# One hybrid decoder block on one core: key halves spread by DMA, sums of h one pair per head, and an earlier emptying of the turned heads

## The chip, the cores and the metric

The program runs on one core of one Trainium2 chip. The metric is the device time of the whole program in microseconds, the median of several executions. Besides these times there is a profile of one execution, with a record of every instruction on every engine: TensorE (PE, with its weight loads shown apart as PEld), VectorE (DVE), ScalarE (ACT), GpSimd (POOL), and SyncE (SP), which issues nearly all DMAs.

## The reference, cut to what matters

The block works on 1024 positions of width 1024, all in float32. The part that the change touches is the differential attention with its four heads:

```python
h = rms_norm(x, g_mix)
proj = h @ w_in                       # q1, q2, k1, k2, va, qr, kr, vr, gr, gate_a, gate_r
s1 = einsum(q1, k1) * scale + bias    # per head, 64 wide, causal, ALiBi
s2 = einsum(q2, k2) * scale + bias
a  = (softmax(s1) - lam * softmax(s2)) @ va
a  = rms(a) * g_diff_sub * (1 - lam_init)
...
merged = sigmoid(gate_a) * (a @ w_diff_proj) + sigmoid(gate_r) * (r @ w_ret_proj)
x = x + merged @ w_out
...
x = x + (silu(zg) * zu) @ w_down      # zg, zu: causal depthwise convolution of rms_norm(x) @ w_up
```

## The kernel before

**Numbers in two halves.** A float32 operand of a matmul is kept as a rounded high half (`hi`, type fp32r) and the rest (`lo`). A product is the sum of three matmuls, hi·hi, hi·lo and lo·hi. ACT makes the high half by a copy, DVE or POOL makes the low half by a subtraction. The normalized input h lies transposed in 16 tiles `hT[0][k]`, `hT[1][k]` (high and low halves, k from 0 to 7).

**Queries and keys.** For each head h, `queries_keys(h)` runs two products over all of h, one for the queries and one for the keys, each in two halves c of 512 positions (`gemm`, PSUM tag "g" with two buffers). The product's 128 rows hold q1 and q2 of the head, or k1 and k2, 64 rows each. For the scores, the kernel stacks the two halves of the query on the 128 partitions: `qs[0]` holds q1's high half on partitions 0 to 63 and its low half on 64 to 127; `qs[1]` has q2, turned over. A score is then two matmuls, against a tile with the key's high half on both groups of 64 partitions and one with the key's low half on both. `keys` (L476 to L481) makes those tiles from PSUM: for each of k1 and k2, ACT copies the high half to the low and the top 64 partitions (L479), and DVE subtracts twice, once for each group of partitions (L481).

**Attention.** `attention(h)` runs over eight blocks of 128 queries in the order 3, 7, 6, 5, 4, 2, 1, 0. For each, PE makes scores (L502, PSUM tag "x"), DVE adds the bias and takes the minimum (L507), ACT takes the exponential (L512), DVE mixes the two softmaxes (L515 to L517), PE turns the result by transposes (L525), ACT empties it (L527), PE multiplies by the values (L530), and DVE and ACT finish (L532, L534).

**Sums of h.** `h_sums` (L571) is the preparation for a seven-product scheme that later replaces eight block products. For each of four pairs of blocks (k, k + 4) it adds high and low halves (two additions of 128x1024, L288 through `plus`), forms four differences of 128x512 (L285 through `sub`) in tiles `ta` (tag "vo", 6 buffers) and `tb` (tag "br", 9 buffers), and stores both to DRAM as `t_saved` (two DMAs, L584). `h_side` (L588) later loads the stored parts back and splits them; with p = 5 it puts them over the second half of `hT[.][k]`.

**What sets the order.** In this first part the order on each engine's queue, the SP queue of DMAs included, is worked out when the program is built, by a planner: program order gives the priority, a simulated time line says when an instruction can run, and later work fills gaps. A tile's buffer has to be free before its first writer may run. Within the shared tags the tiles of the sums stand in program order between those of the heads: an even head takes six "br" buffers (two queries, four keys), an odd head two "br" and four "c". The outer loop (L707 to L717) calls `attention(h)`, `queries_keys(h + 1)`, after head 0 also `h_sums()`, then the last head and the products for the retention's queries and keys (`retention_product`, tag "br" as well), which keep PE supplied during attention.

**Steps by hand.** From L727 on, the work of PE, DVE, ACT and POOL is ordered by hand: `issue` walks a list of steps. For each step i it issues loads for step i + 9, sums for i + 4, the high half of the weights for i + 3 (ACT), the low half for i + 2 (DVE), and then step i's `pre` list, its matmuls `mm`, and its `post` list. A step is twelve matmuls of 128x512. In the last of the steps for the gates, the attention's output is turned: `turn_a(h)` (L795) makes eight transposes into two PSUM buffers of tag "b" (there are two), and `finish_a(h)` (L799) empties them, two ACT copies for the high half (L803) and two DVE operations for the low half (L805). `n_gates` is 84: `turn_a(0..3)` stand in the `post` lists of steps 77 to 80 and `finish_a(0..3)` in those of steps 78 to 81 (L902 to L906). The products with `w_diff_proj` (`ps_pa`) begin at step 84.

Of the kernel before, what the change touches and what calls it, by code (L numbers as in the profile page):

```python
# [11 lines left out]
F32 = mybir.dt.float32  # L12
F32R = mybir.dt.float32r
AF = mybir.ActivationFunctionType
ALU = mybir.AluOpType
# [120 lines left out]
def hybrid_block(ctx: ExitStack, tc: tile.TileContext, units, xT, wall, lams, pars, consts, dist, out):  # L136
    nc = tc.nc
# [5 lines left out]
    def t4(tag, name, dt=F32, shape=(P, 1024)):  # L143
        return tp.tile(list(shape), dt, tag=tag, name=name, bufs=BUFS[tag])
# [137 lines left out]
    HK = KB // 2  # L282

    def sub(out, a, b, engine=nc.vector):
        engine.tensor_tensor(out, a, b, op=ALU.subtract)  # L285

    def plus(out, a, b, engine=nc.vector):
        engine.tensor_tensor(out, a, b, op=ALU.add)  # L288

    def copy(out, a):  # L290
        nc.scalar.activation(out, a, AF.Copy)  # L291
# [34 lines left out]
    steps, index, behind = [], {}, []  # L326
# [26 lines left out]
    with ExitStack() as first:  # L353
# [3 lines left out]
        def psum(tags, name):  # L357

            turn[0] += 1
            return pp.tile([P, 512], F32, tag=tags[turn[0] % len(tags)], name=name)  # L360
# [8 lines left out]
        for k in range(KB):  # L369
# [3 lines left out]
            for c in range(0, S, 512 if k == 0 else S):  # L373
                cs = slice(c, c + (512 if k == 0 else S))
# [8 lines left out]
            for st in range(NST):  # L383
                a = [t[:, st * P : (st + 1) * P] for t in u[k]]
                b = [t[:, k % 2 * 256 : (k % 2 + 1) * 256] for t in w]
# [16 lines left out]
        for st in range(NST):  # L402
            ps = psum("gx", f"ps_va1_{st}")[:, 0:256]
# [18 lines left out]
        for k in range(KB):  # L422
            xt = t4("s", f"xn{k}")
            nc.sync.dma_start(out=xt, in_=xT[k * P : (k + 1) * P, :])
            for c in range(2):
                cs = slice(c * 512, (c + 1) * 512)
# [23 lines left out]
        def gemm(name, tags, nm, done, engine=nc.vector):  # L450

            w = weight(name, engine=engine)
            for c in range(2):
                ps = psum(tags, f"ps{nm}_{c}")
                channel_major(ps, w, of_h, KB, c)
                done(slice(c * 512, (c + 1) * 512), ps)
# [4 lines left out]
        low, top = slice(0, HD), slice(HD, P)  # L461

        def queries_keys(h):
            sc = -(HD**-0.5) / SLOPES[h]
            qs = [t4("br", f"q{m}_{h}", F32R) for m in range(2)]
            tag = "c" if h % 2 else "br"
            ks = [[t4(tag, f"k{e}{m}_{h}", F32R) for e in range(2)] for m in range(2)]

            def queries(cs, ps):
                for q, a, b in ((qs[0], low, top), (qs[1], top, low)):  # L470
                    nc.scalar.activation(q[a, cs], ps[a], AF.Copy, scale=sc)
                    nc.vector.scalar_tensor_tensor(
                        q[b, cs], ps[a], sc, q[a, cs].bitcast(F32), op0=ALU.mult, op1=ALU.subtract
                    )

            def keys(cs, ps):  # L476
                for (kh, kl), a in zip(ks, (low, top)):
                    for b in (low, top):
                        nc.scalar.activation(kh[b, cs], ps[a], AF.Copy)  # L479
                    for b in (low, top):  # L480
                        nc.vector.tensor_tensor(kl[b, cs], ps[a], kh[a, cs].bitcast(F32), op=ALU.subtract)  # L481

            gemm(("q", h), "g", f"q{h}", queries, nc.gpsimd)
            gemm(("k", h), "g", f"k{h}", keys, nc.gpsimd)
            return qs, ks
# [58 lines left out]
        def spill(name, i, t):  # L544
            if name == "vr":
                spilled[name, i] = values[:, i, :]
            elif name in ("qr", "kr"):
                spilled[name, i] = queries_and_keys[:, i + (0 if name == "qr" else 2), :]
            else:
                spilled[name, i] = dram.tile([P, S], F32, name=f"{name}_saved{i}")  # L550
            nc.sync.dma_start(out=spilled[name, i], in_=t)
# [6 lines left out]
        def retention_product(name, p):  # L558
            t = t4("br", f"{name}{p}")
            gemm((name, p), "g", f"{name}{p}", lambda cs, ps: copy(t[:, cs], ps), nc.gpsimd)  # L560
            spill(name, p, t)
# [6 lines left out]

        t_saved = []

        def h_sums():  # L571

            for k in range(HK):
                a, b = t4("vo", f"ta{k}"), t4("br", f"tb{k}")
                for t, e in ((a, k), (b, k + HK)):
                    plus(t, hT[0][e].bitcast(F32), hT[1][e].bitcast(F32))
                b11, b12, b21, b22 = a[:, 0:512], a[:, 512:], b[:, 0:512], b[:, 512:]
                sub(b11, b12, b11)
                sub(b12, b22, b12)
                sub(b22, b22, b11)  # L580
                sub(b21, b21, b22)
                t_saved.append([dram.tile([P, S], F32, name=f"t_saved{e}_{k}") for e in range(2)])
                for t, d in zip((a, b), t_saved[k]):
                    nc.sync.dma_start(out=d, in_=t)  # L584
# [3 lines left out]
        def h_side(p, k, tag=None):  # L588

            if tag:  # L590
                t = t4(tag, f"ht{p}_{k}", F32R)
                hi, lo = t[:, 0:512], t[:, 512:]
            else:
                hi, lo = (t[k][:, second_half] for t in hT)
            e, cs = {5: (0, first_half), 7: (0, second_half), 4: (1, first_half), 6: (1, second_half)}[p]
            nc.sync.dma_start(out=lo.bitcast(F32), in_=t_saved[k][e][:, cs])
            split(lo.bitcast(F32), hi, lo)
            h_sides[p, k] = hi, lo
# [109 lines left out]
        for h in range(NH - 1):  # L708
            attention(h, *qk)
            qk = queries_keys(h + 1)  # L710
            if h == 0:
                h_sums()
        attention(3, *qk, (3, 7, 6))
        level = tc.cur_priority
        for name in ("qr", "kr"):
            for p in range(2):
                retention_product(name, p)  # L717
        for k in range(HK):
            h_side(5, k)
        for p, tag in ((6, "br"), (7, "br")):  # L720
# [20 lines left out]
        def at_step(i, *ops):  # L741
            steps[i].post.extend(ops)
# [36 lines left out]
        def scale_heads(o, r):  # L779

            nc.vector.tensor_tensor(o, o, r.rearrange("p (a b) -> p a b", b=1).broadcast_to([P, 8, DV]), op=ALU.mult)
# [113 lines left out]
        n_gates = len(steps)  # L895
# [7 lines left out]
        for h in range(NH):  # L903
            at_step(18 + h, lambda h=h: scale_heads(oa[h], rstd_a[:, h * NST : (h + 1) * NST]))
            at_step(n_gates - 7 + h, partial(turn_a, h))
            at_step(n_gates - 6 + h, partial(finish_a, h))  # L906


        MERGED = ("br",) * 5 + ("s", "s", "vo")
# [47 lines left out]
        for n in range(2 * NH):  # L957
            h, c = n // 2, n % 2
# [610 lines left out]
def build(units, arrays):  # L1569
    import concourse.bacc as bacc  # L1570

    nc = bacc.Bacc("TRN2", target_bir_lowering=False, num_devices=1)
    args = [nc.dram_tensor(f"in_{n}", a.shape, mybir.dt.from_np(a.dtype), kind="ExternalInput").ap() for n, a in arrays.items()]
    out = nc.dram_tensor("out_0", (D, S), F32, kind="ExternalOutput").ap()
    with tile.TileContext(nc, schedule_with_timeline_sim=True) as tc:
        hybrid_block(tc, units, *args, out)
    return nc
# [9 lines left out]
```

## Time and profile before

| | |
|---|---|
| Time, median of 3 executions | 1434.86 us (1434.17 to 1435.17) |
| The profiled execution's own time | 1434.84 us |
| Its span, first to last instruction | 1433.0 us |
| PE busy | 1368.6 us, 96% of the span |
| DVE busy | 1068.0 us, 75% |
| ACT busy | 703.4 us, 49% |
| DMA, mean over the span | 131 GB/s |

The profiled execution is an ordinary one: its time lies within the range of the others, and some 1.8 us of it lie outside the span. A view by windows gives, for a stretch of time, how long each engine was busy, how many instructions it ran, the clock that TensorE was granted (1.00 is full speed) and the share of the DMA engines. A PE that is busy at a clock of 0.5 does half the work. Matmuls overlap in the records, so the pace of PE is read from the distance between starts, not from the length of one.

### The profile page before, as it was taken

To read this page: it belongs to the slowest core of one execution; us is meant where nothing else is said; L and a number is where in the kernel's file an instruction comes from. 1 tells how busy PE (TensorE), PEld (TensorE's weight loads), DVE (VectorE), ACT (ScalarE), POOL (GpSimd) and SP (SyncE) were. 2 spreads that over 40 slices of the span, in tenths; PEclk is the share of its full clock that TensorE was granted. 3 is DMA by queue.
4 is the path that set the end of the run, shared out by engine and by line. 5 is a ranking of instruction groups with operands and counts; after the bars stand their busy time and mean duration, and the time that the engine had idled before them with its cause. 6 is when DMAs were issued, how large, how long until landed. Compare 5 with 4: busy or idle time off the path is not lost.

```text
span 1433.0 us, 18055 instructions
## 1 busy us (share of the span) xinstructions
PE 1368.6 (96%) x6472; PEld 1134.0 (79%) x6472; DVE 1068.0 (75%) x1699; ACT 703.4 (49%) x1318; POOL 154.3 (11%) x92
## 2 busy tenths in 40 slices
PE   7899899989999998999998989999999999999996
PEld 7887788878888886788776767888888888888885
DVE  6759765675655553467968989888988899897876
ACT  6544665564454434221445465455555556444452
POOL 6711001000000000000000012111111112200000
PEclk9999999999999999999989999999999999999997
DMA  7313101314334332635324134434433365943223
GB/s 250 125 45 121 56 16 45 137 70 143 137 125 136 108 110 81 251 138 180 153 100 148 59 113 159 133 122 136 139 126 125 125 228 195 331 165 103 94 90 118
DMA packets 81018, 187.55 MB, mean 131 GB/s; under 512 B 8320, under 2 KB 18944, under 8 KB 80928
## 3 DMA queue, kind: packets, MB, share of 16 engines
q1 hardware_dynamic: 80736, 185.74, 37.8%
q8 instruction: 51, 0.84, 0.2%
q0 software_dynamic: 192, 0.66, 0.1%
q14 instruction: 39, 0.32, 0.1%
HBM read 136.81 MB, written 49.55 MB: 130 GB/s over the span
## 4 chain that ended last, share of the span: by engine, by line
PE 42%; DVE 7%; ACT 1%; issue 1%; DVEq 0%; ACTq 0%
PE up L276 24%; PE wd L276 14%; PE wo L276 4%; DVE wf L285 1%; DVE f L285 1%; DVE x L1461 1%; DVE y L1381 1%; DVE ssum L228 1%; DVE x L1230 1%; DVE x L288 1%; DVE x L285 0%; ACT f L291 0%; DVE zg L288 0%; DVE raw_zg L285 0%; DVE wwo L285 0%
## 5 line engine op out<-in xcount | busy, mean ns | idle before, releaser
L276 PE MATMUL up<-f,wf 128*128 128x512 f32 x1848 | 424.8, 391 | 9.2 <-DVE wf L285 3.4
L276 PEld LDWEIGHTS up<-f,wf 128*128 128x128 f32 x1848 | 345.3, 188 | 88.1 <-DVE wf L285 6.4
L276 PE MATMUL wd<-awd,wwd 128*128 128x512 f32 (+1 forms) x960 | 212.2, 383 | 0.0
L276 PEld LDWEIGHTS wd<-awd,wwd 128*128 128x128 f32 x960 | 176.0, 189 | 35.4 <-issue 0.5
L285 POOL TENSOR_TENSOR t12g<-y 128x512 f32<-128x512 f32 x11 | 19.8, 1796 | 673.3 <-DVE y L1391 538.4
L276 PE MATMUL wo<-awo,wwo 128*128 128x512 f32 x336 | 83.2, 407 | 7.4 <-DVE awo L285 7.1
L276 PEld LDWEIGHTS wo<-awo,wwo 128*128 128x128 f32 x336 | 64.9, 196 | 24.8 <-DVE awo L285 10.1
L512 ACT ACTIVATE s<-s,row 128x512 f32<-128x512 f32 (+7 forms) x64 | 49.5, 773 | 26.7 <-DVE row L507 26.2
L1381 DVE SCALAR_TENSOR_TENSOR y<-zg,par,y 128x1022 f32<-128x1022 f32 (+1 forms) x44 | 58.6, 1333 | 2.9 <-ACT y L1378 2.9
L502 PE MATMUL pss<-k,q 128*128 128x512 f32 (+2 forms) x192 | 52.8, 371 | 5.6 <-DVE row L507 5.5
L288 DVE TENSOR_TENSOR zg<-zg,up 128x512 f32<-128x512 f32 x44 | 30.2, 685 | 37.0 <-PE up L276 34.6
L1381 DVE SCALAR_TENSOR_TENSOR y<-zu,par,y 128x1022 f32<-128x1022 f32 (+1 forms) x44 | 56.1, 1277 | 0.0
L291 ACT ACTIVATE zg<-up 128x512 f32<-128x512 f32 x44 | 26.1, 596 | 58.5 <-PE up L276 58.5
L285 DVE TENSOR_TENSOR awd<-act_in,awd 128x512 fp32r<-128x512 f32 x77 | 53.7, 697 | 0.0
L507 DVE CUSTOM_DVE_ANT_0 s<-pss,dist_t 128x512 f32<-128x512 f32 (+3 forms) x64 | 37.0, 587 | 21.1 <-PE pss L502 19.7
L291 ACT ACTIVATE awd<-act_in 128x512 fp32r<-128x512 f32 x77 | 47.5, 616 | 0.3 <-DVE wf L285 0.2
L276 PE MATMUL ps_pa<-a,wpa 128*128 128x512 f32 x192 | 46.0, 394 | 0.0
L206 PE MATMUL psq<-hT,hi_q 128*128 128x512 f32 x128 | 43.2, 415 | 2.5 <-ACT hi_q L163 1.7
L291 ACT ACTIVATE zu<-up 128x512 f32<-128x512 f32 x44 | 26.2, 596 | 39.2 <-PE up L276 39.1
L276 PE MATMUL ps_pr<-r,wpr 128*128 128x512 f32 x192 | 43.7, 389 | 0.0
L291 ACT ACTIVATE wwd<-wdv 128x512 fp32r<-128x512 f32 x33 | 20.9, 632 | 46.1 <-PE wd L276 37.1
L530 PEld LDWEIGHTS po<-va,at 128*128 128x128 f32 x288 | 38.1, 195 | 6.2 <-ACT at L527 4.1
(367 smaller groups left out, 2822.9 us busy)
## 6 DMA issues: line engine op xcount, KB each, us to landing
act_in<-act SPq DMA_DIRECT2D x77, 256.0 KB, 2.9
act<-y SPq DMA_DIRECT2D x55, 256.0 KB, 2.2
raw_zg<-in_wall SPq DMA_DIRECT2D x22, 512.0 KB, 3.4
raw_zu<-in_wall SPq DMA_DIRECT2D x22, 512.0 KB, 4.1
x<-in_x SPq DMA_DIRECT2D x15, 512.0 KB, 7.8
act<-t12g SPq DMA_DIRECT2D x22, 256.0 KB, 2.0
wdu<-in_wall SPq DMA_DIRECT2D x22, 256.0 KB, 4.8
wdv<-in_wall SPq DMA_DIRECT2D x22, 256.0 KB, 5.7
```

Source lines behind the costliest of these rows:

```text
L206: nc.tensor.matmul(ps, w, a, start=i == 0, stop=i == n - 1)
L228: engine.tensor_tensor(self.ssum, self.ssum, sq, op=ALU.add)
L276: nc.tensor.matmul(ps[:, cols], w[:, x * 512 + at : x * 512 + at + P], a[y][:, cols], start=start and i == 0, stop=stop and i == n - 1, sk ...
L285: engine.tensor_tensor(out, a, b, op=ALU.subtract)
L288: engine.tensor_tensor(out, a, b, op=ALU.add)
L291: nc.scalar.activation(out, a, AF.Copy)
L502: nc.tensor.matmul(ps[:, : max(n, 256)], qs[m][:, i * P : (i + 1) * P], k[:, c : c + max(n, 256)], start=e == 0, stop=e == 1,)
L507: nc.vector.tensor_tensor_reduce(s[:, c : c + n], ps[:, :n], dst_t[:, S - width + c : S - width + c + n], SLOPES[h], low_, op0=ALU.add, op ...
L512: nc.scalar.activation(s[:, :width], s[:, :width], AF.Exp, bias=low_, scale=-1.0, accum_out=z[:, m : m + 1])
L530: nc.tensor.matmul(po, at[:, k * P : (k + 1) * P], va[h][:, kb, :], start=kb == 0, stop=kb == i)
L1230: nc.vector.scalar_tensor_tensor(y, y, gain(1, at), row, op0=ALU.mult, op1=ALU.mult)
L1381: nc.vector.scalar_tensor_tensor(y[side][:, n:], z[:, : S - n], t[:, j : j + 1], y[side][:, n:], op0=ALU.mult, op1=ALU.add)
```

## The change

Three edits, in one diff. The keys' high half and low half are made once, on the 64 partitions where the product lies, and two DMAs on SP's queue bring each of them to the other 64 partitions. `h_sums` takes the pairs that it is to do: one pair after each of the heads 0, 1 and 2, and the last one after the products for the retention's queries and keys. `finish_a(h)` moves from the `post` list of its step to the `pre` list of the same step, so that it is issued ahead of that step's matmuls and of what follows them.

```diff
             def keys(cs, ps):
-                for (kh, kl), a in zip(ks, (low, top)):
-                    for b in (low, top):
-                        nc.scalar.activation(kh[b, cs], ps[a], AF.Copy)
-                    for b in (low, top):
-                        nc.vector.tensor_tensor(kl[b, cs], ps[a], kh[a, cs].bitcast(F32), op=ALU.subtract)
+                for (kh, kl), a, b in zip(ks, (low, top), (top, low)):
+                    nc.scalar.activation(kh[a, cs], ps[a], AF.Copy)
+                    nc.vector.tensor_tensor(kl[a, cs], ps[a], kh[a, cs].bitcast(F32), op=ALU.subtract)
+                    for t in (kh, kl):
+                        nc.sync.dma_start(out=t[b, cs].bitcast(F32), in_=t[a, cs].bitcast(F32))
...
-        def h_sums():
-
-            for k in range(HK):
+        def h_sums(*blocks):
+
+            for k in blocks:
...
         for h in range(NH - 1):
             attention(h, *qk)
             qk = queries_keys(h + 1)
-            if h == 0:
-                h_sums()
+            h_sums(h)
         attention(3, *qk, (3, 7, 6))
         level = tc.cur_priority
         for name in ("qr", "kr"):
             for p in range(2):
                 retention_product(name, p)
+        h_sums(HK - 1)
         for k in range(HK):
             h_side(5, k)
...
             at_step(n_gates - 7 + h, partial(turn_a, h))
-            at_step(n_gates - 6 + h, partial(finish_a, h))
+            steps[n_gates - 6 + h].pre.append(partial(finish_a, h))
```

## The prediction

> **What bounds the kernel now.** The page comes first: which engine is full over the span.
>
> ```profile
> span 1433.0 us, 18055 instructions
> PE 1368.6 (96%) x6472; PEld 1134.0 (79%) x6472; DVE 1068.0 (75%) x1699; ACT 703.4 (49%) x1318; POOL 154.3 (11%) x92
> ```
>
> PE is busy for 96%, so time is won only where PE stands still or runs at a lower clock. The view by windows over the attention shows where that is (columns: PE, PEld, DVE, ACT, POOL busy, granted clock, DMA):
>
> ```profile
> 120.00:140.00 20.00, 17.95 (x85) 14.41 (x85) 18.17 (x37) 8.72 (x17) 3.36 (x2) 0.91 0.36 131
> 140.00:160.00 20.00, 16.33 (x89) 13.67 (x88) 17.29 (x48) 12.47 (x36) 1.41 (x1) 0.83 0.23 80
> 160.00:180.00 20.00, 20.00 (x108) 17.15 (x107) 13.71 (x31) 13.30 (x28) 2.41 (x1) 1.00 0.09 27
> 180.00:200.00 20.00, 18.90 (x124) 16.52 (x123) 14.43 (x48) 13.04 (x35) 2.87 (x1) 1.00 0.09 27
> 200.00:220.00 20.00, 20.00 (x104) 16.88 (x103) 14.88 (x36) 12.68 (x34) 2.30 (x1) 1.00 0.00 1
> 240.00:260.00 20.00, 20.00 (x114) 17.38 (x113) 7.79 (x30) 9.84 (x26) 2.40 (x1) 1.00 0.07 28
> 280.00:300.00 20.00, 17.58 (x100) 13.83 (x100) 16.28 (x43) 16.04 (x35) 0.00 (x0) 1.00 0.39 142
> 300.00:320.00 20.00, 18.30 (x103) 15.43 (x102) 15.45 (x41) 11.80 (x34) 0.00 (x0) 1.00 0.27 93
> ```
>
> From 120 to 160 us PE loses 2.05 + 3.67 = 5.7 us idle, and by the clock another 0.09 x 20 + 0.17 x 20 = 5.2 us: 10.9 us together. DVE is busy for 35.5 of these 40 us. What it does there, apart from attention, are the sums of h and the keys. The windows of the sums' two lines, L285 and L288, over 99 to 150 us (first number behind the length: DVE busy), then a PE row of the same stretch, then the keys' groups:
>
> ```profile
> 99.00:150.00 51.00, 12.85 (x16) 0.00 (x0) 0.94 0.31 107
> 99.00:150.00 51.00, 10.70 (x8) 0.94 0.31 107
> ```
> ```profile
> 146.69 0.84 PE L502 MATMUL pss<-k,q 128*128 128x256 f32 x4 [0.90 <-DVE row L507]
> ```
> ```profile
> L479 ACT ACTIVATE k<-psk x32: 575/594/600, 85.6 to 221.2; 64x512 fp32r<-64x512 f32 x32
> L481 DVE TENSOR_TENSOR k<-psk,k x32: 672/688/695, 86.9 to 222.6; 64x512 fp32r<-64x512 f32 x32
> ```
>
> L285 and L288 cost 12.85 + 10.70 = 23.6 us of DVE, 5.9 us a pair. The PE row is typical: scores wait for DVE's emptying of the previous ones. The second place is the turning of the heads, in the time line of PE:
>
> ```profile
> 544.86 2.88 PE L276 MATMUL pa_gt<-ht,wgt 128*128 128x512 f32 x12
> 547.58 2.88 PE L276 MATMUL pb_gt<-hT,wgt 128*128 128x512 f32 x12
> 550.30 1.03 PE L787 MATMUL pta<-cst,oa 128*128 128x128 f32 x8
> 551.09 3.01 PE L276 MATMUL pa_gt<-ht,wgt 128*128 128x512 f32 x12
> 556.67 1.77 PE L787 MATMUL pta<-cst,oa 128*128 128x128 f32 x8 [2.57 <-DVE a L805]
> 558.10 4.26 PE L276 MATMUL pb_gt<-hT,wgt 128*128 128x512 f32 x12
> 564.40 1.31 PE L787 MATMUL pta<-cst,oa 128*128 128x128 f32 x8 [2.05 <-DVE a L805]
> 565.47 2.99 PE L276 MATMUL pa_gt<-ht,wgt 128*128 128x512 f32 x12
> 570.51 1.77 PE L787 MATMUL pta<-cst,oa 128*128 128x128 f32 x8 [2.05 <-DVE a L805]
> 571.94 4.17 PE L276 MATMUL pb_gt<-hT,wgt 128*128 128x512 f32 x12
> 575.95 2.89 PE L276 MATMUL pa_gt<-ht,wgt 128*128 128x512 f32 x12
> 579.62 3.01 PE L276 MATMUL pa_gt<-ht,wgt 128*128 128x512 f32 x12 [0.78 <-DVE z_gt L288]
> 582.47 0.84 PE L276 MATMUL ps_pa<-a,wpa 128*128 128x512 f32 x3
> ```
>
> A free step lasts 2.72 us (544.86 to 547.58). The steps with a turn last 7.01, 7.37 and 6.47 us: PE waits for `finish_a` of the head before, and runs on at half clock, as these windows show:
>
> ```profile
> 557.36:560.77 3.41, 3.41 (x10) 2.87 (x11) 0.51 (x1) 0.00 (x0) 0.00 (x0) 0.50 0.01 1
> 571.01:574.42 3.41, 3.41 (x12) 2.76 (x11) 0.70 (x2) 1.38 (x2) 0.00 (x0) 0.50 0.10 41
> ```
>
> **Edit 3, the turned heads.** ACT's copies of `finish_a` stand today behind the step's own output, which ends with its matmuls, and the next turn needs both PSUM buffers back:
>
> ```profile
> 554.14 0.60 ACT L619 ACTIVATE z_gt<-pa_gt 128x512 f32<-128x512 f32 x1 [2.96 <-PE pa_gt L276]
> 555.15 1.26 ACT L803 ACTIVATE a<-pta,gd 128x512 fp32r<-128x512 f32 x2
> 555.87 1.41 DVE L805 SCALAR_TENSOR_TENSOR a<-pta,gd,a 128x512 fp32r<-128x512 f32 x2 [4.08 <-ACT a L803]
> ```
>
> Put ahead, the copies start when the transposes end (551.3), DVE follows 0.7 us behind, and both buffers are empty near 551.3 + 0.7 + 1.4 = 553.4, before the step's matmuls end at 551.09 + 2.72 = 553.8. Nothing is added: two copies and two DVE operations per head move past twelve matmuls and past the step's output copies; no DMA or POOL work is in them. The output copies now stand behind 1.26 us of ACT that run while PE multiplies. In the second of the three steps ACT is later, since two output copies and a weight half (0.60 to 0.63 us each) precede `finish_a(1)`; for this I leave 0.8 us of waiting. From 551.09 to 582.47 are 31.38 us. Needed are 6 x 2.72 = 16.3 us, three turns of 0.79 us (550.30 to 551.09) = 2.4, and the wait ahead of 579.62, which stays (579.62 - 575.95 - 2.72 = 0.95): 19.6, with the 0.8 about 20.4. **Gain 11.0 us**; bounds 8 (each turn still waits about 1 us) and 11.8. The loads behind it are not late: they are issued nine steps ahead, and at 582 us the next product starts without a wait.
>
> Two half-clock windows account for 3.4 us of this. [...]
>
> **Edit 2, the sums.** Three of four pairs, 3 x 5.9 = 17.7 us of DVE, leave 116 to 149 us. With that (and 4 x 0.688 = 2.75 us of keys) DVE falls from 35.5 to about 17 of 40 us, and PE becomes the limit of that stretch. Not all 10.9 us return: the end of a head's attention has no product to fill PE, and head 1's end (180 to 200) loses 1.1 us without any sums. I leave 1.9. **Gain 9.0 us**; bounds 3 and 11. The pairs arrive elsewhere: a pair needs a "br" buffer that is free only when the head before has ended, so they fall near 155 to 175, 200 to 215 and 240 to 265 us of the old count, where PE is full and DVE has 6.3, 5.1 and 12.2 of 20 us free. Per head +5.9 - 2.75 = +3.2 us of DVE. Six operations that can each hold up a score by at most 1.2 us: **cost 0.5 us**, bounds 0 and 4. Their two stores per pair pass the weight loads on SP; each takes 0.33 us to issue:
>
> ```profile
> 109.71 0.33 SPq L196 DMA_DIRECT2D raw_q<-in_wall  x1
> ```
>
> **Edit 1, the keys.** 16 ACT copies (9.5 us) and 16 DVE operations (11.0 us) go; 32 DMAs of 128 KB come. The trace has none of that size within SBUF; the nearest rows:
>
> ```profile
> act<-t12g SPq DMA_DIRECT2D x22, 256.0 KB, 2.0
> ht<-t_saved SPq DMA_DIRECT2D x12, 256.0 KB, 4.4
> ```
>
> I take 2.0 us (a lone store is nearest), at most 4.4; it can't be less than nothing. Their issue costs SP 32 x 0.33 = 10.6 us, spread over 130 us. Head 1's last keys and first scores (the first 512 wide ones after head 0):
>
> ```profile
> 129.17 1.40 DVE L481 TENSOR_TENSOR k<-psk,k 64x512 fp32r<-64x512 f32 x2
> 153.44 1.20 PE L502 MATMUL pss<-k,q 128*128 128x512 f32 x2
> ```
>
> Between them lie 22.9 us, 13.9 if head 0 ends 9 us sooner: the transfers of heads 1 to 3, made in the same way during the head before, are hidden; without that cover each would cost 2 us or more. SP waits for DVE at each; behind it stand the next weight loads, for which ACT waits, with slack of many us. Only head 0 has no slack:
>
> ```profile
> 85.62 1.20 ACT L479 ACTIVATE k<-psk 64x512 fp32r<-64x512 f32 x2 [2.59 <-PE psk L206]
> 90.86 1.07 PE L502 MATMUL pss<-k,q 128*128 128x512 f32 x4
> ```
>
> ACT 85.6 to 86.8, DVE to 87.6, landing at 89.6 (at most 92.0): scores at 90.86 wait 0 to 1.1 us, and if they stand still the half clock could add 1.7. Against it, ACT and DVE are free earlier. **Cost 0**, bounds -1 and 3. [...]
>
> **Sum.** 1434.84 - 11.0 - 9.0 + 0.5 = **1415.3 us**, made against the profiled execution, which agrees with the median (1434.86) to 0.02 us.
>
> **The rivals.**
> - *The attention gives nothing*: the planner lays the sums and scores out anew and the chain of scores, exponential and turn is itself the limit (for it: PE also waits at 180 to 200 without sums; against: DVE is nearly full only at 120 to 160). 1434.84 - 11.0 = 1423.8.
> - *The half clock stays* though the waits go: the four half-clock shares (3.4 + 5.2 us) are not won. 1415.3 + 8.6 = 1423.9. Against it: the windows follow the waits. [...]
> - *Only the attention gains*: `finish_a` still ends late, each turn waits as now. 1434.84 - 8.5 = 1426.3. Against it: DVE idles 4.08 us ahead of it.
> - *More*: freed DVE and ACT also shorten 280 to 320, where PE idles 2.42 + 1.70 us: 1415.3 - 4.1 = 1411.2, with the upper bounds of the gains 1408.
> - *Slower*: the sums' buffers. Pair 1 now stands in "br" ahead of head 3's queries, pair 2 ahead of the retention's products, pair 3 ahead of `h_side`. If the planner runs a pair late, the product behind it can't leave PSUM and PE has no filling, as at 120 to 160, at 10.9 us each. Two such places nearly cancel the gain (1437.1); it turns slower beyond that, with all three: 1415.3 + 32.7 = 1448. Against it: the DVE room above.
> - *It doesn't do what it says*: the planner puts all pairs where they were and the turns wait on another buffer: 1434.8.
>
> **How the numbers follow.** Forecast 0.60; attention gives nothing 0.12; half clock stays 0.05; only attention 0.05; more 0.10; slower 0.05; no effect 0.03. The range 1407 to 1428 holds all but the last two and the low edge of "more": 1407 takes in the upper bounds, 1428 the lower bounds of single terms (8 and 3 give 1424, with 3 to 4 of cost 1428). A measurement of this kernel can tell about 0.2% (2.9 us) from no change; faster by more 0.92, within 0.03, slower 0.05.
>
> **What would show it.** In the trace after: steps between the turns 3.5 to 4.5 us apart and no half clock there; no half clock in the first head's second half and DVE well below full; `t_saved` stores spread over 150 us; the keys' DMAs landing in 2 us with PE full at 91. It is wrong if products of queries or of the retention wait for a buffer, or if PE waits for SP's transfers.

## The result and the profile after

| | time, us | against before |
|---|---|---|
| before, beside it on the same chip | 1434.51 (1431.19 to 1435.17) | |
| changed | 1418.62 (1415.76 to 1420.5) | 0.9884, 95% interval 0.9859 to 0.9909 |
| forecast | 1415.3 (1407 to 1428) | |

The changed kernel is faster by 15.9 us where 19.5 were forecast. Its profiled execution took 1420.5 us, the longest of its four, so the sums over the trace below come out 1.9 us above the median. One of the four executions of `sums_turn_again` below, of 4833 us, is left out of its median and ratio. The page after, its span and its engines:

```profile
span 1418.7 us, 18115 instructions
...
PE 1358.9 (96%) x6472; PEld 1128.3 (80%) x6472; DVE 1057.1 (75%) x1683; ACT 692.0 (49%) x1302; POOL 153.9 (11%) x92
```

PE has as many instructions as before and 9.7 us less busy time, nearly all of it clock: half-clock time over the whole span falls from 46.2 to 28.2 us, worth up to 9.0 (at half clock the 128x512 matmuls start 0.43 us apart, as from 736.4 to 740.6 us before; at full clock 0.23, as from 544.86 to 550.30). DVE and ACT have 16 operations fewer each, the keys' second copies. The attention by windows, columns as in the prediction:

```profile
120.00:140.00 20.00, 20.00 (x116) 17.40 (x114) 11.63 (x29) 8.86 (x19) 2.38 (x1) 1.00 0.36 115
140.00:160.00 20.00, 18.41 (x111) 15.70 (x110) 13.66 (x46) 14.55 (x43) 2.38 (x1) 1.00 0.09 28
160.00:180.00 20.00, 19.20 (x97) 15.91 (x96) 17.94 (x32) 8.65 (x18) 2.40 (x1) 1.00 0.43 131
180.00:200.00 20.00, 17.88 (x116) 15.23 (x116) 15.64 (x51) 14.18 (x40) 2.37 (x1) 1.00 0.09 27
...
280.00:300.00 20.00, 16.23 (x98) 12.94 (x96) 17.60 (x47) 13.11 (x31) 0.00 (x0) 1.00 0.50 181
300.00:320.00 20.00, 18.35 (x103) 15.44 (x103) 16.43 (x42) 12.46 (x36) 0.00 (x0) 1.00 0.28 93
```

From 120 to 160 us the clock is 1.00 in place of 0.91 and 0.83, and DVE is busy for 25.3 of 40 us in place of 35.5. PE idles 1.6 us there in place of 5.7. But it now loses more from 180 to 200 (2.1 us, before 1.1) and from 280 to 300 (3.8 us, before 2.4). The turns, in PE's time line:

```profile
549.12 1.03 PE L787 MATMUL pta<-cst,oa 128*128 128x128 f32 x8
549.91 3.01 PE L276 MATMUL pa_gt<-ht,wgt 128*128 128x512 f32 x12
552.77 1.03 PE L787 MATMUL pta<-cst,oa 128*128 128x128 f32 x8
...
556.38 1.04 PE L787 MATMUL pta<-cst,oa 128*128 128x128 f32 x8
...
560.03 1.03 PE L787 MATMUL pta<-cst,oa 128*128 128x128 f32 x8
...
563.63 2.88 PE L276 MATMUL pa_gt<-ht,wgt 128*128 128x512 f32 x12
567.29 3.01 PE L276 MATMUL pa_gt<-ht,wgt 128*128 128x512 f32 x12 [0.78 <-DVE z_gt L288]
570.15 5.15 PE L276 MATMUL ps_pa<-a,wpa 128*128 128x512 f32 x22
```

The turns stand 3.61 to 3.65 us apart, none waits, and the eight transposes last 1.03 or 1.04 us each time, not up to 1.77. From the first turn to the first product with `w_diff_proj` it is 21.0 us, before 32.2 (550.30 to 582.47).

The attention in three stretches, cut where PE starts a product: the first score; the first product of the retention's queries (`psqr`); the first for its values (`pa_vr`); the first for its gate. Before, then after, the same columns:

```profile
90.86:217.35 126.49, 119.67 (x629) 100.93 (x628) 100.99 (x240) 75.30 (x174) 15.15 (x6) 0.96 0.17 59
217.35:282.05 64.70, 64.70 (x349) 55.56 (x349) 34.04 (x94) 34.30 (x82) 7.94 (x3) 1.00 0.22 76
282.05:335.55 53.50, 49.19 (x261) 40.21 (x260) 39.41 (x97) 32.59 (x80) 0.31 (x1) 1.00 0.35 125
```
```profile
94.53:212.42 117.89, 113.38 (x617) 96.03 (x616) 84.35 (x212) 66.08 (x158) 14.34 (x6) 1.00 0.25 72
212.42:277.59 65.17, 65.17 (x352) 55.94 (x350) 35.39 (x94) 33.17 (x80) 8.42 (x3) 1.00 0.26 89
277.59:334.36 56.77, 50.35 (x271) 41.47 (x270) 44.86 (x110) 33.11 (x82) 0.32 (x1) 1.00 0.41 147
```

The first stretch is 8.6 us shorter, the other two together 3.7 us longer (118.20 to 121.94). PE ran 12 matmuls fewer in the first (629, 617), and they have moved behind the cut: PE is busy there for 1.6 us more (64.70 + 49.19 to 65.17 + 50.35). The other 2.1 us are idle time in the last stretch (4.31 to 6.42 us), where DVE has 5.5 us more to do, as the last pair of sums lies there. The whole, between the two profiled executions: start-up 90.9 to 94.5 (+3.7), first stretch -8.6, late attention +3.7, turns -11.1, all behind them -2.0; sum -14.3, measured 1434.84 - 1420.5 = 14.3. PE's idle time over the three stretches is nearly what it was, 6.82 + 4.31 = 11.1 us before and 4.51 + 6.42 = 10.9 after: in the attention this trace wins the clock's 5.1 us and little else.

### The profile page after: what moved, and what is told of

It is laid out like the page before. It is cut to its first block, busy times and chain, and to the rows that moved or that the text cites. A ratio compares the mean times of both kernels' runs of the same rounds, so it can differ in the third digit from the quotient of the medians.

```text
span 1418.7 us, 18115 instructions
## 1 busy us (share of the span) xinstructions
PE 1358.9 (96%) x6472; PEld 1128.3 (80%) x6472; DVE 1057.1 (75%) x1683; ACT 692.0 (49%) x1302; POOL 153.9 (11%) x92
## 4 chain that ended last, share of the span: by engine, by line
PE 42%; DVE 8%; ACT 2%; issue 1%; DVEq 0%; ACTq 0%
PE up L276 24%; PE wd L276 14%; PE wo L276 3%; DVE wf L285 1%; DVE f L285 1%; DVE x L1461 1%; DVE y L1381 1%; DVE ssum L228 1%; DVE x L288 1%; DVE x L1230 1%; DVE x L285 0%; ACT f L291 0%; DVE zg L288 0%; DVE raw_zg L285 0%; DVE wwo L285 0%
## 5 line engine op out<-in xcount | busy, mean ns | idle before, releaser
L285 POOL TENSOR_TENSOR t12g<-y 128x512 f32<-128x512 f32 x11 | 19.8, 1796 | 661.4 <-DVE y L1391 526.6
L288 DVE TENSOR_TENSOR zg<-zg,up 128x512 f32<-128x512 f32 x44 | 30.1, 685 | 36.6 <-PE up L276 34.3
L285 DVE TENSOR_TENSOR awd<-act_in,awd 128x512 fp32r<-128x512 f32 x77 | 53.7, 698 | 0.0
L507 DVE CUSTOM_DVE_ANT_0 s<-pss,dist_t 128x512 f32<-128x512 f32 (+3 forms) x64 | 37.0, 587 | 10.7 <-PE pss L502 10.2
L276 PEld LDWEIGHTS ps_pr<-r,wpr 128*128 128x128 f32 x192 | 36.0, 188 | 7.5
```

The lines of the kernel that those rows point to most:

```text
L276: nc.tensor.matmul(ps[:, cols], w[:, x * 512 + at : x * 512 + at + P], a[y][:, cols], start=start and i == 0, stop=stop and i == n - 1, sk ...
L507: nc.vector.tensor_tensor_reduce(s[:, c : c + n], ps[:, :n], dst_t[:, S - width + c : S - width + c + n], SLOPES[h], low_, op0=ALU.add, op ...
```

## The experiments

Twelve runs, two of them repetitions, in three groups, each group on one chip beside the kernel before (1433.3, 1433.55 and 1433.6 us). In the tables, "early" is the first of the three stretches above and "late" the two others together, from the trace; half-clock time in brackets where there is some.

### One edit alone, and two without the keys

`turn_alone` is the kernel before with

```diff
-            at_step(n_gates - 6 + h, partial(finish_a, h))
+            steps[n_gates - 6 + h].pre.append(partial(finish_a, h))
```

> Only the third edit: finish_a ahead of its step's matmuls. If the emptying alone held the turns (my theory), the span from the first turn to the product with w_diff_proj falls from 32.2 to about 21.0 us and the time is 11.1 us below the kernel before, ratio 0.992. If the half clock came from elsewhere (rival), only about 7.7 us are won.

`sums_alone` is the kernel before with

```diff
-        def h_sums():
-            for k in range(HK):
+        def h_sums(*blocks):
+            for k in blocks:
...
-            if h == 0:
-                h_sums()
+            h_sums(h)
...
+        h_sums(HK - 1)
```

> Only the second edit: one pair of the sums with each head, keys made as before. My theory: PE's losses at 120 to 160 us (10.9 us) shrink to about 4, and the last pair gives about 3 us back near 280: in all 2 to 6 us below the kernel before, ratio 0.996 to 0.999. Rival (the keys' work on DVE and ACT is what fills the stretch): within 2 us of the kernel before.

`keys_alone` is the kernel before with

```diff
-                for (kh, kl), a in zip(ks, (low, top)):
-                    for b in (low, top):
-                        nc.scalar.activation(kh[b, cs], ps[a], AF.Copy)
-                    for b in (low, top):
-                        nc.vector.tensor_tensor(kl[b, cs], ps[a], kh[a, cs].bitcast(F32), op=ALU.subtract)
+                for (kh, kl), a, b in zip(ks, (low, top), (top, low)):
+                    nc.scalar.activation(kh[a, cs], ps[a], AF.Copy)
+                    nc.vector.tensor_tensor(kl[a, cs], ps[a], kh[a, cs].bitcast(F32), op=ALU.subtract)
+                    for t in (kh, kl):
+                        nc.sync.dma_start(out=t[b, cs].bitcast(F32), in_=t[a, cs].bitcast(F32))
```

> Only the first edit: keys' halves by DMA, sums all with head 0 as before. My theory: 0 to 3 us below the kernel before, since 2.75 us of DVE and 2.4 us of ACT go from the full stretch and the transfers are hidden. Rival: the keys carry the attention's gain, 6 to 9 us below. Other rival: transfers late at head 0, up to 3 us above.

`sums_turn` is the changed kernel with that last edit undone.

> The second and third edit, keys as before. My theory: the time of the changed kernel plus 0 to 3 us (1418.6 to 1422). Rival (keys carry the attention's gain): 1423 to 1426, as for the turn alone.

| kernel | time, us | ratio, 95% interval | early | late | turns |
|---|---|---|---|---|---|
| before (trace) | | | 126.5 (10.2) | 118.2 | 32.2 (6.8) |
| `turn_alone` | 1424.39 | 0.9933 (0.9916 to 0.9950) | 126.5 (10.2) | 120.5 (3.4) | 21.0 |
| `sums_alone` | 1426.85 | 0.9953 (0.9936 to 0.9969) | 118.0 | 120.2 | 32.0 (6.8) |
| `keys_alone` | 1430.86 | 0.9988 (0.9977 to 0.9998) | 125.2 (6.8) | 119.5 | 32.1 (6.8) |
| `sums_turn` | 1415.80 | 0.9879 (0.9861 to 0.9897) | 118.0 | 119.9 | 21.0 |
| changed (trace) | 1418.62 | 0.9884 (0.9859 to 0.9909) | 117.9 | 121.9 | 21.0 |

Two edits make the gain, and each makes its own: the turns are 11 us shorter with or without the others, and the early stretch is 8.5 us shorter with the sums' edit alone. `sums_alone` gained a little more than expected.

One row is a warning. Up to 340 us `turn_alone` has the instructions of the kernel before in the same order on PE, DVE, ACT, POOL and SP, and yet its late stretch took 120.5 us against 118.2: it has a half-clock window of 3.4 us, worth 1.7 us, and PE idles 0.8 us more. Half-clock time has to be taken off before two late stretches are compared, and half a microsecond between them, from one trace each, shows nothing. By its times, `turn_alone` gains 9.6 us (7.2 to 12.0), where its turns give 11.1.

The windows of `sums_alone`, then of `keys_alone`:

```profile
120.00:140.00 20.00, 20.00 (x115) 17.40 (x115) 12.68 (x30) 11.34 (x24) 2.84 (x1) 1.00 0.09 27
140.00:160.00 20.00, 19.16 (x111) 16.02 (x110) 13.73 (x44) 13.33 (x39) 2.38 (x1) 1.00 0.10 28
```
```profile
120.00:140.00 20.00, 16.66 (x95) 14.21 (x93) 19.54 (x31) 7.08 (x15) 5.43 (x2) 1.00 0.43 147
140.00:160.00 20.00, 17.13 (x89) 14.22 (x90) 17.79 (x53) 11.83 (x37) 0.00 (x0) 0.83 0.25 91
```

With the sums spread, the half clock is gone though the keys are made as before; with the keys' edit and the sums in place, DVE is as full as before (37.3 of 40 us) and PE idles 6.2 us. The keys' edit by itself is worth 0.12% (1.7 us), with an interval that barely excludes nothing. On top of the two others it is worth nothing: `sums_turn` was expected 0 to 3 us behind the changed kernel, but it has the shortest time of the group, and the trace has it 2 us ahead in the late stretch.

### Where the late stretch loses it

The theory now: a pair of sums that stands ahead of the retention's products or in the last head costs its vector time there. The rival: that place is limited by the last head's own chain, and it doesn't matter where the pair goes. The changed kernel again, then its last pair without the arithmetic (its two sums and four differences are left out; the high halves of h are stored in their place):

```diff
             for k in blocks:
+                if k == HK - 1:
+                    t_saved.append([dram.tile([P, S], F32, name=f"t_saved{e}_{k}") for e in range(2)])
+                    for e, d in zip((k, k + HK), t_saved[k]):
+                        nc.sync.dma_start(out=d, in_=hT[0][e].bitcast(F32))
+                    return
```

> The changed kernel once more, on the same chip as the three runs beside it. Both theories: 1416 to 1420 us, ratio 0.987 to 0.991.

> The changed kernel without the arithmetic of the last pair of the sums: the high halves of h are stored in their place, so six DVE operations of that pair are left out and its stores can go at once. My theory (the last pair falls into the full stretch near 280 and gives gain back): 3 us below the changed kernel, and the stretch from the first product of the step list to the first product of the silu gate falls from 56.8 to about 53.5 us. Rival (that stretch is longer for another reason, such as the order of the scores): within 1 us of the changed kernel.

The last pair ahead of the last head, in the changed kernel (`pair3_ahead`) and in `sums_turn` (`sums_turn_pair3_ahead`):

```diff
             h_sums(h)
+        h_sums(HK - 1)
         attention(3, *qk, (3, 7, 6))
...
-        h_sums(HK - 1)
```

> The changed kernel with the last pair ahead of the last head's attention, so that its operations fall at 220 to 260 us, where DVE is free for half of the time. My theory: 2 to 3 us below the changed kernel. Rival (a pair costs its DVE time anywhere): within 1 us. Other rival (the pair holds the buffer that the retention's products need): 1 to 5 us above.

> The same place of the last pair, with the keys made twice by ACT and DVE as before the change. If the key transfers give nothing: equal to the run with the last pair ahead, within 2 us. If the halved work on ACT and DVE matters once the last pair is out of the way: 2 to 4 us above it.

| kernel | time, us | ratio, 95% interval | early | late |
|---|---|---|---|---|
| `changed_again` | 1419.26 | 0.9902 (0.9884 to 0.9921) | 118.0 | 122.0 |
| `pair3_stored_only` | 1415.08 | 0.9876 (0.9858 to 0.9894) | 117.9 | 121.9 (3.4) |
| `pair3_ahead` | 1418.07 | 0.9898 (0.9880 to 0.9916) | 117.9 | 122.2 |
| `sums_turn_pair3_ahead` | 1418.95 | 0.9898 (0.9881 to 0.9915) | 118.0 | 122.1 (3.4) |

The 122 us repeat. Leaving out the last pair's arithmetic shortens the late stretch only if its one half-clock window (3.4 us, worth 1.7) is taken off: 120.2, so about 1.8 us for the pair's DVE work. The part that the theory expected to fall to 53.5 us stays at 56.7. `pair3_stored_only` has a median 4.2 us under `changed_again`, but the late stretch is not where it comes from: between the two profiled executions the start-up is 2.5 us shorter (94.8 to 92.3) and the part behind the turns 4.0 us (849.7 to 845.8). Moving the pair gains nothing: the last part falls from 56.8 to 54.3 us, and the part before it grows from 65.2 to 67.9. So these traces go with the rival for this pair: its time is paid wherever it stands near the last head.

The third group asks about pair 2, and about no late pairs at all. The waits of ACT in the changed kernel (total us, times, longest), then its time line:

```profile
ACT qr L291 <- DMA t_saved<-tb: 3.9, 1, 3.9
```
```profile
224.45 0.60 ACT L291 ACTIVATE qr<-psqr 128x512 f32<-128x512 f32 x1 [3.93 <-DMA t_saved<-tb]
```

A retention product's output waits 3.9 us for a "br" buffer that pair 2's store still holds. This was the mechanism of the rival "slower", and it is in the changed kernel, in its repetition and in `pair3_stored_only`, but not in `sums_turn`. `pair2_stored_only` leaves the arithmetic of pair 2 out (two sums, four differences), in the same way as above:

```diff
+                if k == 2:
...
+                    return
```

> The changed kernel without the arithmetic of pair 2: its two sums and two differences are left out, and the high halves of the two blocks are stored in their place, at the same place of the program. The retention's products and the last head took 122.0 us together (122.1 again) against 118.2 before and 119.9 with the keys made twice by the engines. Theory A: the queries' product of the retention waits 3.9 us for pair 2's buffer, and that costs about 2 us: 119.5 to 120.5 us in this stretch, no wait of that copy for the store, 1416.5 to 1417.5 in all. Rival: the copy's wait is covered, and pair 2 costs nothing there: 121.5 to 122.5 us, and the time of the changed kernel, 1418 to 1420.

`three_first` is the changed kernel with two pairs behind head 0, two behind head 1 and none later; `nk_three_first` has the keys made twice by the engines besides:

```diff
-            h_sums(h)
+            h_sums(*((0, 1), (2, 3), ())[h])
...
-        h_sums(HK - 1)
```

> The changed kernel with pairs 0 and 1 behind head 0, 2 and 3 behind head 1, none later. Theory A (the give-back of 3.8 us stems from the pairs that stand in front of the retention's products and in the last head): that stretch is back at 118.2 to 119 us with the keys' own share at most 1.2, the three heads before it stay at 117.9 to 119, and the whole is 1414 to 1416. Rival (a pair costs its vector time wherever PE is fed by the vector engine): the heads before grow by 2 to 4 us, the late stretch shrinks by as much, and the whole stays at 1418 to 1420.

> As three_first, with the keys made twice by the engines as before the change. Theory A: the late stretch is back at 118.2, the three heads before it at 118 to 120: 1412 to 1414, better than the sums and turns alone (0.988 of the time before). Rival: the keys' 11 us of vector time and the second pair meet in the first two heads: these take 120 to 124 us, and the whole 1415 to 1419.

And `sums_turn` once more:

> The sums and the turns of the change with the keys made twice by the engines, once more, beside the others of this call. If the keys' transfers cost time together with the sums, as the traces say (122.0 against 119.9 us in the late stretch): 0.986 to 0.989 of the time before, 2 to 4 us under the changed kernel. If that was chance: 0.989 to 0.991, level with it.

| kernel | time, us | ratio, 95% interval | early | late |
|---|---|---|---|---|
| `pair2_stored_only` | 1415.61 | 0.9869 (0.9851 to 0.9887) | 119.1 | 119.7 |
| `three_first` | 1420.02 | 0.9901 (0.9884 to 0.9918) | 121.4 (3.4) | 121.5 |
| `nk_three_first` | 1424.51 | 0.9931 (0.9915 to 0.9947) | 124.9 (6.8) | 121.6 (3.4) |
| `sums_turn_again` | 1415.82 | 0.9873 (0.9851 to 0.9895) | 118.0 | 120.3 |

*The buffer wait doesn't explain it.* Without pair 2's arithmetic the wait is gone and the late stretch is 2.2 us shorter, as the theory said; but the early one is 1.2 us longer. And in the changed kernel PE is busy for all 65.17 us of the stretch that holds the wait (the row 212.42:277.59): the next products fill it. It stopped ACT, not PE. That ACT's standing still put the last head off isn't excluded by this run; but `pair3_ahead` has no such wait and the same 122.2 us. Both stretches together are 1.0 us shorter than in the changed kernel (239.8 to 238.8), for some 5.2 us of DVE work left out (two operations of 1.22 us, four of 0.69).

*Without late pairs the late stretch doesn't come back.* Theory A's 118.2 to 119 us were missed by both kernels, and the rival's shorter late stretch as well; the rival's longer early one came, 3.5 us in `three_first`. Stretches as above, for `three_first` and then for `sums_turn`:

```profile
91.90:213.29 121.39, 115.29 (x612) 96.19 (x611) 90.88 (x218) 64.18 (x155) 15.65 (x6) 0.99 0.28 87
213.29:277.83 64.54, 64.54 (x347) 55.46 (x346) 31.94 (x88) 33.49 (x83) 7.17 (x3) 1.00 0.28 90
277.83:334.74 56.91, 51.57 (x281) 42.85 (x280) 42.80 (x109) 33.87 (x83) 0.31 (x1) 1.00 0.32 110
```
```profile
94.05:212.06 118.01, 114.31 (x620) 96.25 (x619) 90.48 (x225) 72.01 (x170) 15.09 (x6) 1.00 0.14 45
212.06:276.76 64.70, 64.70 (x350) 55.49 (x349) 36.94 (x97) 33.84 (x82) 7.80 (x3) 1.00 0.23 82
276.76:331.94 55.18, 50.39 (x272) 41.63 (x271) 44.18 (x108) 33.77 (x83) 0.31 (x1) 1.00 0.43 152
```

`three_first` runs 17 matmuls of the first stretch behind the cut (629 to 612), and has 5.34 us of idle PE in its last stretch with no pair in it; before had 4.31, also without a pair. In all four traces shown PE is full while the retention's queries and keys are made, and idle behind them, where the rest of the last head has little to fill its waits: 4.31 us before, 4.79 in `sums_turn`, 5.34 here, 6.42 in the changed kernel. These three have run 9, 17 and 12 matmuls fewer than the kernel before when the cut comes (629 there, 620, 612 and 617 here), so as many more are left behind it, though the idle time doesn't go by that number alone. What PE waits for differs too: the scores' waits for DVE to empty the one before them, over the late stretch (total us, times, longest), of the kernel before, of the changed one and of `sums_turn`:

```profile
PE pss L502 <- DVE row L507: 1.4, 2, 0.9
```
```profile
PE pss L502 <- DVE row L507: 4.2, 6, 1.1
```
```profile
PE pss L502 <- DVE row L507: 1.5, 2, 0.9
```

In the changed kernel three of the six fall between 286 and 290 us, where DVE works without a gap and ends the last pair (at 287.9 us); but `sums_turn` ends its last pair at 285.9 and has only one wait there. So neither theory of this part explains the late stretch. With half-clock time counted at half, it takes 118.2 to 119.9 us in the five traces whose first stretch runs 627 matmuls or more, and 119.9 to 122.2 in the nine others: whether a pair of sums stands in it or not, it is longer, in these traces, when the planner has placed less of the last head by then. That the one causes the other isn't shown, and what moves the planner there stays open.

*Two pairs behind one head are too many.* `nk_three_first` is slower than `sums_turn_again` by intervals that don't touch, and with two pairs a head the keys' edit seems to be worth something (1420.02 against 1424.51 us, intervals that just overlap). What happens there in `nk_three_first`: a window, then a row each of the time lines of PE, DVE and POOL:

```profile
180.00:190.00 10.00, 6.29 (x20) 3.65 (x19) 9.76 (x22) 3.93 (x6) 2.58 (x1) 0.69 0.43 157
```
```profile
185.83 1.86 PE L502 MATMUL pss<-k,q 128*128 128x512 f32 x4 [2.33 <-DVE row L507]
```
```profile
182.86 2.31 DVE L285 TENSOR_TENSOR tb<-tb,ta 128x512 f32<-128x512 f32 x1
```
```profile
182.03 2.58 POOL L164 TENSOR_TENSOR lo_qr<-raw_qr,hi_qr 128x1024 fp32r<-128x1024 f32 x1 [14.09 <-ACT hi_qr L163]
```

DVE is full, one difference of the sums takes 2.31 us, a score waits 2.33 us for DVE, and from 183.77 us on, within that wait, the clock is at half for 6.83 us: the old place's trouble, at head 1.

No kernel that does the whole computation beat `sums_turn` (0.9879 and 0.9873). Its medians are 2.8 and 3.4 us below those of the changed kernel, but the two never ran in one group; by the ratios it is 0.7 and 4.2 us ahead, and the intervals overlap. The traces are plainer: with half-clock time counted at half, the late stretch takes 119.9 to 120.4 us in the five that spread the sums with the keys made by the engines (`sums_alone`, `sums_turn` twice, `sums_turn_pair3_ahead`, `nk_three_first`), and 121.5 to 122.2 in the four that have the keys' edit beside the spread sums and do all of the arithmetic (the changed kernel twice, `pair3_ahead`, `three_first`). That the keys' edit costs about 2 us beside the sums is likely, though the times alone don't settle it; *why* is open. Nobody waits for a transfer, and the planner's order differs in too many places between the two to name one.

## Why the prediction was right, point by point

- **Edit 3** was forecast to gain 11.0 us and gained 11.1 in the traces. The wait of 0.8 us left for the second of the steps did not come, and the one ahead of the last `pa_gt` (0.78) stayed, as forecast.
- **Edit 2** in the attention: forecast 9.0, measured 8.6 in the early stretch, but made up otherwise. The clock's share came back in full (10.2 us at half clock, 5.1 us). DVE fell to 25.3 us of the 40, not to about 17 (the forecast's terms, 35.5 - 17.7 - 2.75, make 15.0): PE gets further there, 227 matmuls in place of 174, and so there is more of the attention's own work for DVE. Of the idle time 2.3 us came back (126.49 - 119.67 = 6.82 to 117.89 - 113.38 = 4.51), not the 3.8 that the forecast amounts to; the ends of the heads, for which 1.9 us were left out, hold more (140 to 160 and 180 to 200). The remaining 1.2 us are work moved behind the cut.
- **The pairs elsewhere** were the mis-sized term: 0.5 us forecast, bounds 0 to 4, and 3.7 measured with the keys, 1.7 to 2.1 without them (`sums_turn`, twice), against one trace of before (by `turn_alone` without its half-clock window each would be 0.6 less). The step that fell short is "six operations that can each hold up a score by at most 1.2 us": scores were held up, by at most 1.1 us, but the late waits of scores for DVE alone grew by 2.8 us (1.4 to 4.2), where 0.5 was allowed. Other waits there shrank, which leaves 2.1 us of idle PE, and 1.6 us of PE work came later, for which the forecast has no term. Whatever of the last head is left over when the retention's queries and keys are done runs with little beside it. So the attention as a whole gained 4.9 us in the trace, not 8.5. In the profiled execution the start-up and the part behind the turns add 1.7 us to that miss (3.7 - 2.0), which is chance; the median, 1.9 us lower, comes out 3.3 us above the forecast. The places were forecast too early for the last pair: 268 to 288 us, not 240 to 265.
- **Edit 1**: cost 0 (bounds -1 and 3) was somewhat too narrow: alone the edit gained 1.7 us (0.3 to 3.3), and beside the others it likely costs about 2. The next rows are of the changed kernel, all instructions that make a key and their landing:

```profile
L481 SPq DMA_DIRECT2D k<-k x32: 461/462/537, 89.9 to 217.1; - x32
L478 ACT ACTIVATE k<-psk x16: 574/592/596, 89.3 to 215.0; 64x512 fp32r<-64x512 f32 x16
L479 DVE TENSOR_TENSOR k<-psk,k x16: 672/688/695, 89.9 to 215.6; 64x512 fp32r<-64x512 f32 x16
...
DMA to landing us min/median/max: 2.2/2.2/4.7
```

  They land in 2.2 us (2.0 assumed, 4.4 as the upper bound, 4.7 the longest), an issue takes 0.46 us and not 0.33, and no engine waits for one: the cover named was there. At head 0, where the forecast saw no slack, the scores were placed differently: four in one go from 90.86 us before, now at 94.53, 96.57, 97.48 and 98.16 with the next head's query product between them, and PE is busy for all of the 9.00 us from 90 to 99.
- **The rival "the half clock stays"** fell: in `turn_alone` the half-clock windows of the turns are gone with the waits of 2.57 and 2.05 us, and nothing else was changed there. In the kernel before, waits of well under a window's 3.41 us came ahead of it, though it did not follow each time: the half clock came behind the waits of 2.57 us and of 2.05 us ahead of 570.51, and not behind the 2.05 us ahead of 564.40. The last section has what tells them apart.
- **The rival "slower"** named the place rightly (pair 2 ahead of the retention's products, a wait for "br") and the price wrongly: 3.9 us of waiting by ACT, nothing by PE. A product of the retention that waits for a buffer was also one of the forecast's own signs of being wrong; it came, and cost PE nothing in that stretch.
- The other 3.7 us between the two profiled executions are in the start-up, ahead of all that the change touches. Windows there, before and after:

```profile
28.00:36.00 8.00, 6.39 (x51) 6.18 (x52) 6.29 (x5) 5.34 (x20) 5.18 (x4) 1.00 0.61 189
64.00:76.00 12.00, 8.93 (x31) 6.90 (x32) 2.19 (x3) 2.74 (x5) 8.53 (x5) 0.86 0.26 87
```
```profile
28.00:36.00 8.00, 5.52 (x33) 5.11 (x32) 6.18 (x6) 4.41 (x7) 6.70 (x4) 0.79 0.59 183
64.00:76.00 12.00, 8.20 (x34) 6.39 (x33) 4.87 (x5) 4.55 (x10) 10.92 (x7) 0.73 0.14 44
```

  Two half-clock windows more fell into this stretch, ahead of the first score. The edits don't decide it: `turn_alone`, whose edit acts from 550 us on, needs 93.4 us up to the first score, `keys_alone` 90.9, the changed kernel 94.5, and `pair3_stored_only`, the same program up to there, 92.3. The 2.0 us won behind the turns aren't the edits' either: near 730 us the clock is at half for 10.2 us before and for 3.4 after.

## What to carry to other kernels

Before work is spread from a full stretch to others, look not only at each engine's share there but at the *last* of the stretches: what runs beside it, and what is left over when that filling ends. A cheap test is to count the matmuls ahead of a fixed product before and after, and to add up PE's idle time over all the stretches that the work can move between. And where two buffers are emptied behind an engine's output work, put the emptying ahead of it: here that is one line and the larger part of the gain.

## What the runs showed of the hardware that was not expected

**Operations of DVE that meet one of POOL.** Three operations of the sums, two differences (L285) and an addition (L288), took longer in the kernel before. DVE's time line, and POOL's:

```profile
108.78 1.46 DVE L285 TENSOR_TENSOR ta<-tb,ta 128x512 f32<-128x512 f32 x1
...
122.01 1.79 DVE L285 TENSOR_TENSOR ta<-tb,ta 128x512 f32<-128x512 f32 x1
...
140.17 2.32 DVE L288 TENSOR_TENSOR ta<-hT,hT 128x1024 f32<-128x1024 f32 x1
```
```profile
107.00 2.69 POOL L164 TENSOR_TENSOR lo_q<-raw_q,hi_q 128x1024 fp32r<-128x1024 f32 x1 [12.56 <-ACT hi_q L163]
120.85 2.40 POOL L164 TENSOR_TENSOR lo_k<-raw_k,hi_k 128x1024 fp32r<-128x1024 f32 x1 [11.17 <-ACT hi_k L163]
139.03 2.38 POOL L164 TENSOR_TENSOR lo_q<-raw_q,hi_q 128x1024 fp32r<-128x1024 f32 x1 [15.79 <-ACT hi_q L163]
```

Each began while a subtraction of POOL was running and ended 0.55, 0.55 and 1.08 us after it, while the same operations take 0.69 and 1.22 us elsewhere: it looks as if DVE stood until POOL was through. An operation that began before POOL's, at 106.73 us, took its usual 0.69. That is 3.0 us of DVE time in the sums before, and the 2.31 us of `nk_three_first` are the same case (0.56 us after POOL's end). In the changed kernel none of the sums' operations is long; the rows of `ta`:

```profile
L288 DVE TENSOR_TENSOR ta<-hT,hT x4: 1211/1216/1218, 113.3 to 281.6; 128x1024 f32<-128x1024 f32 x4
L285 DVE TENSOR_TENSOR ta<-ta x4: 685/686/687, 116.2 to 283.8; 128x512 f32<-128x512 f32 x4
L285 DVE TENSOR_TENSOR ta<-tb,ta x4: 674/685/693, 117.9 to 284.6; 128x512 f32<-128x512 f32 x4
```

The prediction took DVE's 23.6 us for the sums as they stood, with these 3.0 us in them.

**Half-clock time, and how busy PE was just ahead of it.** In all fourteen traces, up to 1390 us, half-clock time comes in lengths of 3.41 us or multiples of it (6.83 and 10.24 us in the kernel before). Laid end to end from one half-clock window on, windows of 3.41 us tell most of it, with PE's busy time as recorded. In the kernel before, the window ahead of 557.36 us is 25% busy and the one ahead of 571.01 is 40%: half clock follows both. The window from 560.77 to 564.18, which holds most of the wait ahead of 564.40, is 46.3% busy, and full clock follows. Over the fourteen traces, from 9 to 1390 us, half clock followed a full-clock window in all 51 cases in which PE was busy for less than 46.3% of it, in 7 of 52 from there to 61.5%, and in none of 5446 above; in the kernel before and the changed one alone it was 9 of 9, none of 10 and none of 774. So in these traces the half clock also came behind a wait well under 3.41 us that fell inside one window: the 2.05 us ahead of 570.51 do, and of the 2.05 us ahead of 564.40 one window has only 1.83.

**The clock and the start.** Half-clock windows in the start-up come and go between executions of an unchanged stretch, which took 90.9 to 94.8 us in these traces, and the part behind the turns, which no edit touches, took 845.8 to 850.6. A difference of 2 us between two versions can't be read from one execution each. The lengths of the stretches between can, once half-clock time is taken off: repeated, they agree to 0.1 to 0.6 us (121.9 and 122.0; 119.9 and 120.3; 118.2 and 118.8 for `turn_alone`).
